# One decoder layer on one core: a Strassen-like pair of K tiles in each column group of the up projection

## The chip, the core and the metric

The kernel runs on one core of a Trainium2 chip. TensorE (PE) multiplies, VectorE (DVE) and ScalarE (ACT) work on SBUF and PSUM, GpSimd (POOL) and the sync engine (SP) here mostly issue DMAs; all DMAs of the core share 16 DMA engines. The metric is the device time of one execution in microseconds; before the change it is 1249.64 us, the median of three runs (1249.38 to 1251.37).

## The reference

One layer on x of shape (1, 256, 2048), float32: two token mixers with an output projection, then a gated MLP with a short causal convolution, then a gated side input. The MLP is what the change touches:

```python
h = rms_norm(x, ffn_norm_g[i])
u = h @ w_up[i]                      # (256, 2048) @ (2048, 11264)
a, g = jnp.split(u, 2, axis=-1)      # 5632 columns each
a = causal_dwconv(a, conv_w[i], conv_b[i])          # width 3, along the sequence
x = x + (jax.nn.gelu(a, approximate=False) * g) @ w_down[i]
gate = jax.nn.sigmoid(rms_norm(x, ple_norm_g[i]) @ w_ple_gate[i])
x = x + gate * (p[i].astype(x.dtype) @ w_ple_proj[i])
```

## The kernel before

**Precision.** Every weight block is loaded as float32 (`raw`), and split into a high part (`hi`, an ACT cast to a shorter float format, line 960) and a low part (`lo = raw - hi`, DVE, line 961). The left operand is split in the same way ahead of time. A product is three matmuls: left-high x hi, left-high x lo, left-low x hi, each with a 128 x 128 left block and a 128 x 512 right block, summed in one PSUM bank.

**The up projection.** 11 column groups q of 512 columns of a and the same 512 of g. A group goes over the 16 K tiles of 128 rows; one K tile is a *unit*: a 512 KB load (2 x 512 columns), a split, and 2 token halves x 2 column halves x 3 = 12 matmuls into four PSUM banks (lines 1248 to 1250). The prediction counts a group's units u0, u1 and so on. In the last unit the banks close one after the other; ACT scales them by `rstd2` into the SBUF tile EZ (`up_rows`, line 860), DVE transposes EZ into Y in two passes (`up_turn`, line 182), and POOL moves Y back into EZ, columns now on partitions, by 16 small DMAs (`move`, line 188). The convolution, the GELU, the product with g, its split and, for some pairs, the sums for the down projection (tile Sp, lines 839 to 846) follow as six jobs, `up_act`, hung behind units of the next group.

**Buffers.** There are 3 load buffers (`RAW`) and 4 slots for split parts (`PARTS`). `run_units` loads ahead as buffers come free (a buffer is free when the low part of its old content is computed) and splits at most 4 units ahead (6 in the down phase, where more tiles are free). All loads are issued by SP, in the program's order: a load that waits holds up those behind it.

**The down projection** runs in two halves of 1024 output columns over 22 pairs of K tiles. Pairs named in `SEVEN` use seven block products instead of eight (`seven`): sums of left blocks come from HBM (`sums`), sums of right blocks are made by DVE. Before the change the first half has eight such pairs (`SEVEN[1:]`), the second nine. In the first half loads may also use tiles that are free by then: EZ, Y (`ring`), the pT tile. The residual x stays in the SBUF tile xs from the mixers until the down projection adds to it.

The order of instructions within each engine is set by a scheduler that goes by estimated times and dependences; it may move a load or a matmul ahead of others that come earlier in the code.

## Time and profile before

| what | us |
|---|---|
| median of the runs | 1249.64 |
| the profiled execution | 1248.63 |
| its span | 1246.5 |
| PE busy | 1238.5 |
| DVE busy | 824.3 |
| ACT busy | 685.7 |
| up projection, first to last matmul start | 431.5 to 910.9 |

The span is what the profile covers of the execution; 2.1 us lie around it. Busy times are sums over the span. A matmul's listed time overlaps that of the next, so the distance between starts is what counts. In rows of a timeline the columns are start, duration, engine, line, operation, tiles and shapes, and in brackets the engine's idle time before the row and what ended it.

### The profile page before, as it was taken

To read this page: it belongs to the slowest core of one execution; us is meant where nothing else is said; L and a number is where in the kernel's file an instruction comes from. 1 tells how busy PE (TensorE), PEld (TensorE's weight loads), DVE (VectorE), ACT (ScalarE), POOL (GpSimd) and SP (SyncE) were. 2 spreads that over 40 slices of the span, in tenths; PEclk is the share of its full clock that TensorE was granted. 3 is DMA by queue.
4 is the path that set the end of the run, shared out by engine and by line. 5 is a ranking of instruction groups with operands and counts; after the bars stand their busy time and mean duration, and the time that the engine had idled before them with its cause. 6 is when DMAs were issued, how large, how long until landed. Compare 5 with 4: busy or idle time off the path is not lost.

```text
span 1246.5 us, 16075 instructions
## 1 busy us (share of the span) xinstructions
PE 1238.5 (99%) x5665; PEld 1043.7 (84%) x5665; DVE 824.3 (66%) x1024; ACT 685.7 (55%) x950; POOL 245.0 (20%) x457
## 2 busy tenths in 40 slices
PE   9999999999999999999999999999999999999998
PEld 7999988888888888888888888888887888888887
DVE  6455566664565655665676576667669998998653
ACT  7565454554554544655565465556556555566542
POOL 2001166512313202202202220220220000050000
PEclk9999999999999999999999999999999999999999
DMA  8766878765667768778877878887897885786560
GB/s 256 196 187 185 231 213 225 199 206 161 185 191 220 215 189 223 206 219 239 233 226 223 231 235 223 233 238 222 216 309 278 281 288 197 251 270 227 176 211 34
DMA packets 133121, 272.67 MB, mean 219 GB/s; under 512 B 14841, under 2 KB 29809, under 8 KB 133041
## 3 DMA queue, kind: packets, MB, share of 16 engines
q1 hardware_dynamic: 117616, 245.99, 65.6%
q0 software_dynamic: 15040, 25.50, 7.2%
q8 instruction: 44, 0.72, 0.2%
q14 instruction: 36, 0.29, 0.1%
q10 hardware_dynamic: 385, 0.16, 0.0%
HBM read 245.89 MB, written 6.83 MB: 203 GB/s over the span
## 4 chain that ended last, share of the span: by engine, by line
PE 92%; DMA 3%; issue 3%; DVE 1%; ACT 0%; POOL 0%; SPq 0%; DVEq 0%; ACTq 0%; POOLq 0%
PE tg L302 13%; PE tg L303 13%; PE tg L304 13%; PE up L1250 12%; PE up L1249 12%; PE up L1248 12%; DMA raw<-in_w_down_dram 2%; PE dnP L1010 1%; PE dnP L1011 1%; PE dnP L1009 1%; PE dn(1, 0)_8622 L1009 1%; PE dn(0, 0)_8614 L1009 1%; PE dn(1, 0)_8622 L1010 1%; PE dn(0, 0)_8614 L1011 1%; PE dn(0, 1)_8618 L1009 1%
## 5 line engine op out<-in xcount | busy, mean ns | idle before, releaser
L961 DVE TENSOR_TENSOR lo<-raw,hi 128x1024 fp32r<-128x1024 f32 x222 | 271.1, 1222 | 177.6 <-ACT hi L960 176.8
L960 ACT CAST hi<-raw 128x1024 fp32r<-128x1024 f32 x222 | 233.4, 1051 | 253.5 <-DMA raw<-in_w_up_dram 109.3
L273 DVE TENSOR_TENSOR lo<-raw,hi 128x1024 fp32r<-128x1024 f32 (+3 forms) x153 | 177.8, 1163 | 154.6 <-ACT hi L271 154.2
L1250 PE MATMUL up<-hi,x2T 128*128 128x512 f32 x704 | 274.0, 389 | 0.0
L1249 PE MATMUL up<-lo,x2T 128*128 128x512 f32 x704 | 273.9, 389 | 0.0
L1248 PE MATMUL up<-hi,x2T 128*128 128x512 f32 x704 | 270.0, 389 | 0.0
L271 ACT CAST hi<-raw 128x1024 fp32r<-128x1024 f32 (+3 forms) x153 | 153.0, 1000 | 155.3 <-PE tg L304 116.4
L303 PE MATMUL tg<-lo,hT 128*128 128x512 f32 (+2 forms) x480 | 181.5, 378 | 0.0
L302 PE MATMUL tg<-hi,hT 128*128 128x512 f32 (+2 forms) x480 | 180.8, 382 | 0.0
L304 PE MATMUL tg<-hi,hT 128*128 128x512 f32 (+2 forms) x480 | 180.3, 377 | 0.0
L1249 PEld LDWEIGHTS up<-lo,x2T 128*128 128x128 f32 x704 | 132.2, 188 | 27.6
L1248 PEld LDWEIGHTS up<-hi,x2T 128*128 128x128 f32 x704 | 132.1, 188 | 27.3
L1250 PEld LDWEIGHTS up<-hi,x2T 128*128 128x128 f32 x704 | 132.1, 188 | 27.3
L188 POOL DMA_DIRECT2D EZ<-Y x176 | 93.3, 537 | 173.0 <-DVE Y L182 98.5
L304 PEld LDWEIGHTS tg<-hi,hT 128*128 128x128 f32 x480 | 90.1, 188 | 12.5
L303 PEld LDWEIGHTS tg<-lo,hT 128*128 128x128 f32 x480 | 90.2, 188 | 11.8 <-DVE lo L273 0.4
L302 PEld LDWEIGHTS tg<-hi,hT 128*128 128x128 f32 x480 | 89.7, 188 | 11.8
L188 POOL DMA_DIRECT2D x3s<-x3s x32 | 16.9, 536 | 168.1 <-PE dn(0, 1)_8618 L1011 159.9
L304 PE MATMUL tg<-hi,catT 128*128 128x512 f32 x128 | 49.9, 390 | 0.0
L302 PE MATMUL tg<-hi,catT 128*128 128x512 f32 x128 | 49.8, 391 | 0.0
L303 PE MATMUL tg<-lo,catT 128*128 128x512 f32 x128 | 49.8, 389 | 0.0
L846 POOL DMA_DIRECT2D sums<-Sp x9 | 5.2, 577 | 224.2 <-DVE Sp L845 224.2
(610 smaller groups left out, 1873.5 us busy)
## 6 DMA issues: line engine op xcount, KB each, us to landing
raw<-in_w_up_dram SPq DMA_DIRECT2D x176, 512.0 KB, 5.0
raw<-in_w_in_dram SPq DMA_DIRECT2D x71, 512.0 KB, 4.2
raw<-in_w_down_dram SPq DMA_DIRECT2D x44, 512.0 KB, 5.5
raw<-in_w_in_dram SPq DMA_DIRECT2D x40, 432.0 KB, 3.8
raw<-in_w_out_dram SPq DMA_DIRECT2D x32, 512.0 KB, 4.7
EZ<-Y POOLq DMA_DIRECT2D x176, 64.0 KB, 5.7
w2raw<-in_w_down_dram SPq DMA_DIRECT2D x20, 512.0 KB, 6.3
S<-sums SPq DMA_DIRECT2D x17, 512.0 KB, 5.3
```

The lines of the kernel that those rows point to most:

```text
L188: pool.dma_start(out=c[32 * b : 32 * b + 32, a::4], in_=y[32 * a : 32 * a + 32, :, b])
L271: act.copy(hi, raw[:, :w])
L273: dve.tensor_sub(lo, raw[:, :w], f32(hi))
L302: pe.matmul(o, ah, hi[:, i, :], start=first, stop=False)
L303: pe.matmul(o, ah, lo[:, i, :], start=False, stop=False)
L304: pe.matmul(o, al, hi[:, i, :], start=False, stop=last)
L960: act.copy(hi, raw)
L961: dve.tensor_sub(lo, raw, f32(hi))
L1009: pe.matmul(o, ah, hi, start=first, stop=False)
L1248: pe.matmul(o, ah, hi[:, n], start=k == 0, stop=False)
L1249: pe.matmul(o, ah, lo[:, n], start=False, stop=False)
L1250: pe.matmul(o, al, hi[:, n], start=False, stop=k == KD - 1)
```

## The change

In ten of the eleven column groups (q > 0) the first two K tiles are taken as one 256-deep block and multiplied with seven block products instead of eight. Left: four sums of blocks of `x2` (made once, in `up_sums`, kept in a part of the tile uC that is not yet in use, `S_up`). Right: the pair's 1 MB of weights is loaded into the first half of xs (`B_up`) by three DMAs, DVE makes sums of its blocks in the second half (`T`), and the pair's splits take three and a half passes of 1024 instead of two. The four units with the products stand at u6 to u9 of the group, which now has 18 units: six plain ones, these four, eight plain ones. Three products go into the group's own banks; four (`upP`) go into banks of their own, are added up by DVE in `z_up` (also in xs), scaled by ACT, and added to EZ by two DVE passes ahead of the transposes.

Since xs is used, x is stored to HBM (`kept_x`, 2 MB) in group 0 and read back by four DMAs in the first down half; until then xs also gives four more load buffers (`x0` to `x3`) for the first 20 units of the down phase. The first down half has seven pairs with seven products (`SEVEN[2:]`) instead of eight. The six jobs of the last group are hung three units apart, and EZ and Y become load buffers later.

```diff
+    kept_x = kp.tile([P, NT, D], F32, name="kept_x")
...
+        S_up = uC[:, KF - KD - 10 : KF - KD - 8].rearrange("p k n -> p (k n)").rearrange("p (i c) -> p i c", c=256)
+        B_up = xs[:, 0]
+        z_up = xs[:, 1].rearrange("p (i c) -> p i c", c=512)
+
+        def move_x(out, i=0):
+            def f():
+                if out:
+                    nc.sync.dma_start(out=kept_x, in_=xs)
+                else:
+                    c = slice(i * 512, (i + 1) * 512)
+                    nc.sync.dma_start(out=xs[:, :, c], in_=kept_x[:, :, c])
+            return f
...
-        def up_turn():
+        def up_turn(q):
             y = Y.rearrange("p (t b c) -> p t b c", t=NT, b=4)
             for t in range(NT):
+                if q > 0:
+                    dve.tensor_add(EZ[:, t], EZ[:, t], xs[:, 1, t * BLK : (t + 1) * BLK])
                 square(y, t, 0, EZ[:, t])
             move(y, Z)
...
-                    room.update(late=2, pT=1, e0=1, e1=1, ring=1)
-                    late.update(gate=gate, free=i + LAST_UP + 1, hi=v[:, 0:2], lo=v[:, 2:4],
+                    room.update(late=2, pT=1, e0=1, e1=1, ring=1, x0=1, x1=1, x2=1, x3=1)
+                    used["pT"] = used["raw"] + 1
+                    late.update(gate=gate, x=i + 20, free=i + 26, hi=v[:, 0:2], lo=v[:, 2:4],
...
+            def seven():
+                B = B_up
+                b22, b21 = B[:, BLK : BLK + 512], B[:, BLK + 512 : 2 * BLK]
+                pb = {}
+
+                def load(j):
+                    c = slice(q * 512, (q + 1) * 512)
+                    nc.sync.dma_start(out=B[:, 0:BLK].rearrange("p (h c) -> p h c", h=2), in_=w[0, :, :, c])
+                    nc.sync.dma_start(out=b22, in_=w[1, :, 1, c])
+                    nc.sync.dma_start(out=b21, in_=w[1, :, 0, c])
+
+                def split1(hi, lo):
+                    part(half(hi, 0), half(lo, 0), half(B, 0))
+
+                T = xs[:, 1]
+
+                def sums(*_):
+                    dve.tensor_sub(T[:, 0:BLK], B[:, 512 : 512 + BLK], B[:, 0:BLK])
+                    dve.tensor_sub(half(T, 2), b22, half(T, 0))
+                    dve.tensor_sub(half(T, 3), b21, half(T, 2))
+
+                def split2(hi, lo):
+                    part(hi, lo, T[:, 0:BLK])
+
+                def split3(hi, lo):
+                    part(hi, lo, T[:, BLK : 2 * BLK])
+
+                def split4(hi, lo):
+                    part(hi, lo, B[:, BLK : 2 * BLK])
...
+                def fn1(hi, lo):
+                    alone(1, left(0, 0), half(hi, 0), half(lo, 0))
+
+                def fn2(hi, lo):
+                    alone(5, S(1), half(hi, 0), half(lo, 0))
+                    alone(7, S(3), half(hi, 1), half(lo, 1))
+
+                def fn3(hi, lo):
+                    alone(6, S(2), half(hi, 0), half(lo, 0))
+                    three(st["b"][1, 0], *left(1, 1), half(hi, 1), half(lo, 1))
+
+                def fn4(hi, lo):
+                    three(st["b"][0, 1], *S(4), half(hi, 0), half(lo, 0))
+                    three(st["b"][0, 0], *left(1, 0), half(hi, 1), half(lo, 1))
+                    z_ = z_up
+                    act.copy(z_[:, 0], pb[1])
+                    dve.tensor_add(z_[:, 1], pb[6], z_[:, 0])
+                    dve.tensor_add(z_[:, 2], pb[7], z_[:, 1])
+                    dve.tensor_add(z_[:, 1::2], pb[5].unsqueeze(1).broadcast_to([P, 2, 512]), z_[:, 1:3])
+                    for t in range(NT):
+                        r = rstd2[:, t : t + 1]
+                        act.activation(z_[:, 2 * t : 2 * t + 2], z_[:, 2 * t : 2 * t + 2], AF.Copy, scale=r)
...
-            return [unit(k) for k in range(KD)]
+            us = [unit(k) for k in range(first, KD)]
+            if q == 0:
+                return us
+            se, sums = seven()
+            with_after(us[2], sums)
+            return us[:6] + se + us[6:]
...
-        us += down(0, "aux", "mm", sums_done(0), add_rest(0), {}, FIRST, SEVEN[1:])
+        with_after(us[6], move_x(True))
+        with_after(us[8], up_sums)
+        us += down(0, "aux", "mm", sums_done(0), add_rest(0), {}, FIRST, SEVEN[2:])
...
-                at = (8, 9, 10, 11, 12, 13) if q < KF // 4 - 1 else (6, 7, 8, 9, 10, LAST_UP)
-                with_after(us[KD * (q + 1) + at[i]], job)
+                if q < KF // 4 - 1:
+                    with_after(plains[q + 1][i], job)
+                else:
+                    with_after(us[first_late + 10 + 3 * i], between(job))
+        for i in range(4):
+            with_after(us[first_late + 34 + 5 * i], between(move_x(False, i)))
```

How the scheduler places it, at three points of the fifth column group (q = 4). Its units are 64 to 79 before the change and 70 to 87 after it; the number behind raw, hi and lo is the unit's.

First SP's queue in the middle of the group, before the change: the loads of u10 to u14.

```order
L946 DMA raw74_0_5439<-in_w_up_dram 128x2x512
L946 DMA raw75_0_5457<-in_w_up_dram 128x2x512
L946 DMA raw76_0_5475<-in_w_up_dram 128x2x512
L946 DMA raw77_0_5493<-in_w_up_dram 128x2x512
L946 DMA raw78_0_5511<-in_w_up_dram 128x2x512
```

And after it, the loads of u10 to u14 again (raw80 to raw84):

```order
L969 DMA raw80_0_5432<-in_w_up_dram 128x2x512
L969 DMA raw81_0_5454<-in_w_up_dram 128x2x512
L969 DMA raw82_0_5472<-in_w_up_dram 128x2x512
L1296 DMA xs_84<-in_w_up_dram 128x2x512
L1297 DMA xs_84<-in_w_up_dram 128x512
L1298 DMA xs_84<-in_w_up_dram 128x512
L969 DMA raw83_0_5549<-in_w_up_dram 128x2x512
L969 DMA raw84_0_5563<-in_w_up_dram 128x2x512
```

The three loads of the next group's pair (into xs) stand between those of u12 and u13.

Second DVE's queue at the start of the group, from the low part of u2 on, before the change:

```order
L961 TENSOR_TENSOR lo66_5320<-raw66_0_5253,hi66_5319 128x1024
L182 STREAM_TRANSPOSE Y_4007<-EZ_4006 128x8x4x32 x2
L961 TENSOR_TENSOR lo67_5360<-raw67_0_5274,hi67_5359 128x1024
L961 TENSOR_TENSOR lo68_5382<-raw68_0_5305,hi68_5381 128x1024
L961 TENSOR_TENSOR lo69_5400<-raw69_0_5323,hi69_5399 128x1024
```

And after it, again from the low part of u2 (lo72) on:

```order
L986 TENSOR_TENSOR lo72_5384<-raw72_0_5317,hi72_5383 128x1024
L855 TENSOR_TENSOR Sf_5356<-Y_4008,Sf_5356 128x128
L885 TENSOR_TENSOR EZ_4007<-EZ_4007,xs_84 128x1024 x2
L986 TENSOR_TENSOR lo73_5429<-raw73_0_5338,hi73_5428 128x1024
L183 STREAM_TRANSPOSE Y_4008<-EZ_4007 128x8x4x32
L1306 TENSOR_TENSOR xs_84<-xs_84 128x1024
L857 TENSOR_TENSOR Sp_5357<-Sf_5356,Sp_5357 128x4x128
L183 STREAM_TRANSPOSE Y_4008<-EZ_4007 128x8x4x32
L986 TENSOR_TENSOR lo74_5451<-raw74_0_5369,hi74_5450 128x1024
L986 TENSOR_TENSOR lo75_5469<-raw75_0_5387,hi75_5468 128x1024
```

Between the low parts of u2 and u4 (lo72, lo74) there are now two adds, a sum of B and the split of Sp besides the two transposes and u3's low part.

Third PE's queue at u4 (unit 74), after the change:

```order
L1275 MATMUL up00_5434<-hi74_5450,x2T0_3577 128x512
L1275 MATMUL up10_5435<-hi74_5450,x2T0_3577 128x512
L1275 MATMUL up01_5436<-hi74_5450,x2T0_3577 128x512
L1275 MATMUL up11_5437<-hi74_5450,x2T0_3577 128x512
L1275 MATMUL upP1_5541<-hi76_5489,x2T0_3577 128x512
L1276 MATMUL up00_5434<-lo74_5451,x2T0_3577 128x512
```

The unit's four matmuls with the high part, and one of u6 (hi76), now stand ahead of the first with the low part; at u13 it is the four alone. Before the change a unit's low part was used from its second matmul on.

More of the change, by code (lines that the diff above doesn't have):

```diff
@@ L45 @@
 FRONT = (8, 4, 4)
-LAST_UP = 11
 @with_exitstack
@@ L902, in may @@
             def may(t):
-                return (t not in ("pT", "ring") or j < late["gate"]) and (t not in ("e0", "e1", "ring") or now[0] > late["free"])
+                return (t not in ("pT", "ring") or j < late["gate"]) and (t not in ("e0", "e1", "ring") or now[0] > late["free"]) and (t[0] != "x" or j < late["x"])
             return sorted((t for t in room if taken.count(t) < room[t] and may(t)), key=lambda t: used.get(t, -1))
@@ L946, in load @@
                     nc.sync.dma_start(out=raw[:, : kb * n].rearrange("p (k n) -> p k n", k=kb), in_=src)
+                    last["load"] = traced()
                     self.raws.append(raw)
@@ L1228, in behind, with between, f @@
             return f
+        def between(hook):
+            def f():
+                with tc.issue_after(last["hi"]), tc.issue_after(last["lo"]), tc.issue_after(last["load"]):
+                    hook()
+            return f
         def with_after(u, hook):
@@ L1237, in up_group, with three, left, S @@
             st = {}
+            first = 2 if q > 0 else 0
+            def three(o, ah, al, hi, lo, start=False, stop=False):
+                pe.matmul(o, ah, hi, start=start, stop=False)
+                pe.matmul(o, ah, lo, start=False, stop=False)
+                pe.matmul(o, al, hi, start=False, stop=stop)
+            def left(k, t):
+                a = x2[:, k]
+                return a[:, t * P : (t + 1) * P], a[:, 256 + t * P : 256 + (t + 1) * P]
+            def S(i):
+                return S_up[:, i - 1, 0:P], S_up[:, i - 1, P:256]
@@ L1246, in fn @@
                             o = st["b"][t, n]
[L1247 to L1250 removed]
+                            three(o, *left(k, t), hi[:, n], lo[:, n], k == first, k == KD - 1)
                             if k == KD - 1:
```

37 lines of the change are left out of this document (26 added, 11 removed).

## The prediction

> **What bounds the kernel now.** I read the profile's page first, then the chain of waits, then windows of single column groups, then the timelines of DVE and ACT at one group's end, and last the DMA rows. The page:
>
> ```profile
> span 1246.5 us, 16075 instructions
> PE 1238.5 (99%) x5665; PEld 1043.7 (84%) x5665; DVE 824.3 (66%) x1024; ACT 685.7 (55%) x950; POOL 245.0 (20%) x457
> PEclk9999999999999999999999999999999999999999
> ```
>
> PE is busy throughout, at the full granted clock. Whether it also never waits, the chain of waits tells (start, duration, what); the same three matmuls stand in each group of the up projection:
>
> ```profile
> 508.74 0.68 PE up L1248 x3
> 552.26 0.68 PE up L1248 x3
> ...
> 856.90 0.68 PE up L1248 x3
> ```
>
> Nine starts lie 43.52 us apart. A group is 192 matmuls, so one costs 43.52 / 192 = 0.2267 us (the 389 ns of the groups' table overlap each other) and a unit of 12 costs 2.72. Not one group waits. The windows (stretch, length, busy PE, PEld, DVE, ACT, POOL, clock, DMA share, GB/s) show what stands behind that:
>
> ```profile
> 552.20:595.80 43.60, 43.60 (x194) 36.12 (x193) 27.87 (x33) 23.88 (x28) 9.06 (x17) 1.00 0.77 227
> 910.90:1030.00 119.10, 117.88 (x520) 97.30 (x519) 106.63 (x119) 69.85 (x81) 8.51 (x16) 1.00 0.83 282
> ```
>
> So a saved matmul in the up projection is worth its 0.2267 us as long as the split weights arrive in time. How much time they have, one unit shows: the group beginning at 606.50, its unit u5 (units counted from 0), due at 606.50 + 5 x 2.72 = 620.10.
>
> ```profile
> 606.50 0.39 PE L1248 MATMUL up<-hi,x2T 128*128 128x512 f32 x1
> 612.13 1.05 ACT L960 CAST hi<-raw 128x1024 fp32r<-128x1024 f32 x1 [1.66 <-PE up L1250]
> 613.22 1.22 DVE L961 TENSOR_TENSOR lo<-raw,hi 128x1024 fp32r<-128x1024 f32 x1 [1.49 <-ACT hi L960]
> 620.32 0.39 PE L1249 MATMUL up<-lo,x2T 128*128 128x512 f32 x1
> ```
>
> The low part is ready at 614.44 and first used at 620.32: a **lead** of 5.88 us. It cannot be larger: the ACT pass waited for PE to free the parts slot of u1 (four slots), at 606.50 + 5.44 = 611.94, and the low part was done 2.50 later. The three units between give 8.16 us; the lead is that, less 2.28.
>
> **The change part by part.** *Matmuls.* Ten groups need 21 products instead of 24 for one pair of K tiles (30 fewer), the first down half 3 more: 27 x 0.2267 = **-6.12 us**.
>
> *DVE and ACT.* Prices, from the groups by shape:
>
> ```profile
> L1057 DVE TENSOR_TENSOR raw<-raw 128x512 f32<-128x512 f32 x8 | 5.5, 689 | 0.1
> L776 DVE TENSOR_TENSOR xs<-tg,xs 128x512 f32<-128x512 f32 x8 | 5.1, 682 | 0.0
> L182 DVE STREAM_TRANSPOSE Y<-EZ 128x1024 f32<-128x1024 f32 x22 | 26.1, 1224 | 5.7 <-ACT EZ L860 5.7
> L872 ACT COPY Y<-EZ 128x1024 f32<-128x1024 f32 x11 | 11.5, 1046 | 1.6 <-DMA EZ<-Y 1.6
> ```
>
> Back to back a 1024 pass takes 1.14 and a 512 pass 0.6 (the overlap is in the next rows: two transposes in 2.37). Per group DVE gains 1.5 splits (1.7), the B sums (1.14 + 2 x 0.6), the three product sums (2 x 0.6 + 1.14) and two adds into EZ (2.3): 8.7 us on 27.9, 36.6 of 42.84. ACT gains about 4.4 (1.5 high passes, one 512 copy, two 1024 passes). DVE at 106.63 of 119.10 kept PE supplied in the down half, so volume alone does not decide: **place** does, twice in each group.
>
> *Place one, the load of u13.* The seven products are u6 to u9 with 3, 6, 6 and 6 matmuls, 4.76 us in all. They use up four parts slots as any units do, so at u10 the three units between give 18 x 0.2267 = 4.08 and the lead is 1.8; at u11 3.2, at u12 4.5. In SP's queue the three loads of the *next* group's B (1.05 MB) now stand ahead of u13's load. They wait until u9's split has read the old B: slot freed at 16.32 (u5's end), so done at 18.8 at the earliest; u13's load follows at about 20.0, when u10's split has freed its buffer. What the DMA engines give in such a stretch, the windows show with POOL's moves of EZ (first row) and without (second); below them the issues of the first stretch (last column: median us to landing) and, over two and a half groups, the landing times of up loads:
>
> ```profile
> 611.00:625.00 14.00, 14.00 (x63) 11.59 (x62) 5.63 (x5) 4.21 (x4) 7.01 (x14) 1.00 1.00 241
> 626.00:650.00 24.00, 24.00 (x107) 19.89 (x106) 19.00 (x25) 16.86 (x21) 0.58 (x1) 1.00 0.73 225
> ...
> raw<-in_w_up_dram SPq DMA_DIRECT2D x5, 512.0 KB, 7.3
> EZ<-Y POOLq DMA_DIRECT2D x14, 64.0 KB, 6.0
> ...
> DMA to landing us min/median/max: 3.8/4.9/7.9
> ```
>
> With moves in flight the engines are full at 241 GB/s; without, 225 / 0.73 = 308 GB/s would fill them. A load alone lands in 3.8, of which 0.52 MB / 308 is 1.7, so 2.1 is fixed and B's data start at 20.9. The moves begin after the transposes:
>
> ```profile
> 604.98 2.41 ACT L860 ACTIVATE EZ<-up,rstd_ffn 128x512 f32<-128x512 f32 x4
> 606.85 2.37 DVE L182 STREAM_TRANSPOSE Y<-EZ 128x1024 f32<-128x1024 f32 x2 [0.52 <-ACT EZ L860]
> 609.14 1.18 DVE L961 TENSOR_TENSOR lo<-raw,hi 128x1024 fp32r<-128x1024 f32 x1
> 609.52 5.30 POOL L188 DMA_DIRECT2D EZ<-Y  x10 [6.26 <-DVE Y L182]
> 619.04 1.08 POOL L188 DMA_DIRECT2D EZ<-Y  x2 [0.25 <-DMA EZ<-Y]
> ```
>
> Transposes end at 609.22, the last move lands at 620.12 + 6.0: 16.9 us later. After the change the transposes end 5 to 8 us later in the group (next place), so moves run until 25 to 28, and about 0.35 of their 1.05 MB is still to come at 20.9. Upper bound: (1.05 + 0.52 + 0.35) MB / 241 GB/s = 8.0, landing 28.9, split (1.05 + 1.22) at 31.2; u13 is at 29.24 and needs the low part after four high matmuls, at 30.15: **1.05 late**. Behind u13's high pass ACT then has the two 1.05 passes that scale the products before u14's: about 0.4 more. Lower bound: 1.57 MB / 308 = 5.1, split at 28.3: 1.8 early, no stall.
>
> [...]
>
> *Place two, the group's end.* DVE had two transposes between u2's and u3's splits. Now it has add, add, u3, transpose, B sum, Sp (0.6), transpose, u4: 7 x 1.14 + 0.6 = 8.6. Begun at T + 0.3 as now (T the group's start; the third eviction), u4 is done at 8.9 and needed at 10.88 + 5 x 0.2267 = 12.0: hidden. But it begins only when u2's split is done. Three load buffers turn over in 3.8 + 1.05 + 1.22 + 0.1 = 6.2 us against 8.16 of PE, so at best 0.66 us of lead is regained per unit, 4.6 between u13 and u2, less the convolution passes in that stretch. A lead of 2 at u2 puts its split at T + 4.35 and u4's at 12.95: **0.9 late**; a lead of 4 leaves 1.1 to spare. I take 0.4.
>
> Sum per group: 0 to 2.4, I take 1.6, near the upper end, since the full window with moves is the nearest row. Groups 1 and 2 live on the 5.88 that they inherit; eight remain: **+12.8 us**.
>
> *Keeping x.* The 2 MB store stands ahead of u6's load in group 0, and B's first load waits for it in SP's queue, with u7's load behind. The rows for a store to HBM (512 KB) and for the one stall of the down half:
>
> ```profile
> 908.43 5.53 DMA sums<-Sp
> ...
> 951.31 1.05 ACT hi L960
> 952.41 0.50 PE dn(1, 0)_7768 L1009
> ```
>
> At 308 GB/s it is 2.1 + 6.8 = 8.9, at the store's rate (0.52 MB in 5.53 - 2.1) 2.1 + 13.7. Loads stand 8.16 + 5.88 = 14 us ahead of PE and need 7, so 7 is spare; u7's load would have waited 5.4 of the 8.9 anyway and B's 0.8 MB adds 2.6: 0 to 6 us, I take **+1**.
>
> *Down.* PE waits 1.2 of 119.1 there, at 952.41, behind DVE. The last group's convolution passes are spread wider, one pair (3.5 x 1.14 + 4 x 0.6 = 6.4 of DVE against 2.3) is plain, and the first fourteen units are plain; x's return less one load of sums is 1.6 MB, 5 us of DMA in a window with 17% of 119 free. -1.2 to +3, I take **-0.7**.
>
> 1248.63 (the profiled execution) - 6.12 + 12.8 + 1 - 0.7 = 1255.6; that execution lies 1.0 under the median of the runs, so **1256.5**.
>
> **The rivals.** *The loads keep up (0.22).* If the moves are through before B arrives, every place is hidden: 1249.6 - 6.1 + 0.5 - 0.7 = 1243, faster. For it: a DMA share of 0.77 over a group, and from u5's to u9's split SP has nothing new to issue, so moves run alone for a while. Against it: the full window, and 1.8 us of lead at u10. It decides when u13's load lands within 9 us of B's issue (30.15 - 1.05 - 1.22 - 18.8). *Stalls of about the saving (0.08):* 0.7 a group, 1247 to 1252. *DVE cannot catch up (0.08):* the adds wait so long that place two costs 2 us beside place one's 1.4, 3.4 x 8 = 27: 1266 to 1273. *That it saves nothing* is excluded: the order has 27 matmuls fewer.
>
> **How the numbers follow.** The forecast (1.1 to 2.4 a group, 1252 to 1264) has 0.62. About 0.2% (2.5 us) is what a measurement here can tell. Faster 0.22, same 0.08, slower 0.70. The forecast's own range is 1252 to 1264; 1242 to 1267 takes in the first rival.
>
> **What would show it.** Groups 1 and 2 near 42.84 us and later ones 44 to 45; ACT's high passes in the middle of a group waiting for up weights, DVE's at u4 with no idle time ahead; a load at u13 of 7 us or more. Wrong, if all groups keep 42.84, or if PE waits mostly at u6 to u10.

## The result, and the profile after

| what | before | after |
|---|---|---|
| median of the runs, us | 1250.94 (14 runs) | 1251.9 (14 runs) |
| the profiled execution, us | 1248.63 | 1249.73 |
| its span, us | 1246.5 | 1248.0 |
| up projection, first to last matmul start, us | 479.4 | 482.3 |

The ratio of the runs is 1.0011, with a 95% interval of 0.9997 to 1.0026: no difference that these runs can tell. The 27 saved matmuls (6.1 us) are there, and something has eaten them.

The page of the changed kernel, its span, its busy times, and the shares of the chain that ended last (the last row is the kernel before's shares):

```profile
span 1248.0 us, 16158 instructions
PE 1237.1 (99%) x5638; PEld 1037.5 (83%) x5638; DVE 900.1 (72%) x1124; ACT 719.1 (58%) x999; POOL 244.1 (20%) x457
...
PE 75%; DVE 12%; DMA 7%; issue 3%; ACT 3%; SPq 0%; ACTq 0%; DVEq 0%
...
PE 92%; DMA 3%; issue 3%; DVE 1%; ACT 0%; POOL 0%; SPq 0%; DVEq 0%; ACTq 0%; POOLq 0%
```

PE alone no longer makes the end: 22% of the chain now runs over DVE, loads and ACT, where it was 4%. The windows of single column groups (stretch, length, busy PE, PEld, DVE, ACT, POOL, clock, DMA share, GB/s; each stretch runs from one group's last matmul to the next one's) say where:

```profile
476.53:519.37 42.84, 42.84 (x190) 35.47 (x189) 30.97 (x33) 28.87 (x34) 8.46 (x16) 1.00 0.75 215
519.37:562.44 43.07, 43.07 (x192) 35.66 (x190) 34.16 (x38) 27.23 (x32) 8.44 (x16) 1.00 0.74 218
562.44:605.28 42.84, 42.84 (x191) 35.42 (x189) 35.42 (x43) 26.97 (x33) 9.03 (x17) 1.00 0.78 228
605.28:650.39 45.11, 44.04 (x190) 35.15 (x189) 36.85 (x44) 28.43 (x34) 9.04 (x17) 1.00 0.77 225
...
782.76:827.05 44.29, 43.51 (x190) 35.24 (x189) 36.64 (x44) 28.18 (x34) 9.04 (x17) 1.00 0.78 228
```

A group without a stall now lasts 189 x 0.2267 = 42.84 us. Groups 1 to 3 (counted from 0) do (one matmul more falls into the second stretch). The six groups from 605.28 to 870.74 take 265.46, which is 8.42 more than 6 x 42.84; with 0.5 us in group 10 and 0.7 in group 0 (of which the kernel before loses 0.2 as well) the stalls are **9.6 us** (the expectations below say 9.5).

They sit at two places, u4 and u13 with its neighbour u14. Group 8, DVE from the low part of u2 to that of u4, then PE at u4 (start, duration, engine, line, operation, tiles; in brackets the idle time ahead and what ended it):

```profile
785.35 1.22 DVE L986 TENSOR_TENSOR lo<-raw,hi 128x1024 fp32r<-128x1024 f32 x1
786.49 0.28 DVE L855 TENSOR_TENSOR Sf<-Y,Sf 128x128 f32<-128x128 f32 x1
786.81 2.36 DVE L885 TENSOR_TENSOR EZ<-EZ,xs 128x1024 f32<-128x1024 f32 x2
789.08 1.22 DVE L986 TENSOR_TENSOR lo<-raw,hi 128x1024 fp32r<-128x1024 f32 x1
790.22 1.24 DVE L183 STREAM_TRANSPOSE Y<-EZ 128x1024 f32<-128x1024 f32 x1
791.38 1.18 DVE L1306 TENSOR_TENSOR xs<-xs 128x1024 f32<-128x1024 f32 x1
792.48 0.68 DVE L857 TENSOR_TENSOR Sp<-Sf,Sp 128x512 fp32r<-128x512 f32 x1
793.08 1.24 DVE L183 STREAM_TRANSPOSE Y<-EZ 128x1024 f32<-128x1024 f32 x1
794.24 2.32 DVE L986 TENSOR_TENSOR lo<-raw,hi 128x1024 fp32r<-128x1024 f32 x2
```

```profile
788.20 0.39 PE L1276 MATMUL up<-lo,x2T 128*128 128x512 f32 x1
...
794.32 0.39 PE L1275 MATMUL upP<-hi,x2T 128*128 128x512 f32 x1
795.48 0.50 PE L1276 MATMUL up<-lo,x2T 128*128 128x512 f32 x1 [0.78 <-DVE lo L986]
```

DVE does not rest for a moment. From the end of u2's low part (786.57) to the end of u4's (about 795.43) it needs 8.86 us. PE, left alone, goes from its first use of u2's low part to that of u4's in two units and four matmuls, 6.35. So a lead of 2.5 us at u2 would hide this; it is 788.20 - 786.57 = 1.63. The bracket shows less than the loss: 795.48 - 794.32 = 1.16 between two starts is 0.93 too much, and the matmuls after it start a little late as well, 1.07 in all. Loss is read from starts.

At u13 the load is what comes last. SP's issues and ACT's passes in the same group:

```profile
797.79 0.54 SPq L1296 DMA_DIRECT2D xs<-in_w_up_dram  x1
803.09 0.33 SPq L1297 DMA_DIRECT2D xs<-in_w_up_dram  x1
803.46 0.43 SPq L1298 DMA_DIRECT2D xs<-in_w_up_dram  x1
804.22 0.55 SPq L969 DMA_DIRECT2D raw<-in_w_up_dram  x1
```

```profile
811.29 1.05 ACT L984 CAST hi<-raw 128x1024 fp32r<-128x1024 f32 x1 [6.35 <-DMA raw<-in_w_up_dram]
812.24 2.19 ACT L1344 ACTIVATE xs<-xs,rstd_ffn 128x1024 f32<-128x1024 f32 x2
814.33 1.98 ACT L984 CAST hi<-raw 128x1024 fp32r<-128x1024 f32 x2
```

The DMA engines in the stretch of u13's load (40 slices of 804.2 to 812.0, busy share in tenths, and the sums):

```profile
DMA  9999699799798999999999999999999999999999
...
DMA packets 1165, 2.24 MB, mean 287 GB/s; under 512 B 192, under 2 KB 192, under 8 KB 1163
```

The engines are full. u13's load, issued at 804.22 behind the next group's pair, is in at 811.2: 7.0 us. Its low part is just in time (a lead of 0.16 us); u14's high pass then waits for the two scaling passes, and PE loses 0.3 us there.

In the first down half PE's wait is gone:

```profile
914.00:1033.00 119.00, 119.00 (x527) 98.54 (x526) 107.21 (x122) 70.48 (x84) 9.07 (x17) 1.00 0.84 292
```

### The profile page after: what moved, and what is told of

It is laid out like the page before. It is cut to its first block, busy times and chain, and to the rows that moved or that the text cites. A ratio compares the mean times of both kernels' runs of the same rounds, so it can differ in the third digit from the quotient of the medians.

```text
span 1248.0 us, 16158 instructions
## 1 busy us (share of the span) xinstructions
PE 1237.1 (99%) x5638; PEld 1037.5 (83%) x5638; DVE 900.1 (72%) x1124; ACT 719.1 (58%) x999; POOL 244.1 (20%) x457
## 4 chain that ended last, share of the span: by engine, by line
PE 75%; DVE 12%; DMA 7%; issue 3%; ACT 3%; SPq 0%; ACTq 0%; DVEq 0%
PE tg L303 13%; PE tg L304 13%; PE tg L305 13%; DMA raw<-in_w_up_dram 6%; DVE lo L986 6%; PE up L1276 5%; PE up L1277 5%; PE up L1275 4%; ACT hi L984 2%; DVE Y L900 1%; DVE Y L183 1%; PE dnP L1036 1%; PE dnP L1037 1%; PE dnP L1038 1%; DVE EZ L885 1%
## 5 line engine op out<-in xcount | busy, mean ns | idle before, releaser
L986 DVE TENSOR_TENSOR lo<-raw,hi 128x1024 fp32r<-128x1024 f32 (+1 forms) x206 | 243.3, 1191 | 96.4 <-ACT hi L984 95.6
L984 ACT CAST hi<-raw 128x1024 fp32r<-128x1024 f32 (+1 forms) x206 | 209.9, 1030 | 155.7 <-DMA raw<-in_w_up_dram 103.3
L1276 PE MATMUL up<-lo,x2T 128*128 128x512 f32 x644 | 252.3, 392 | 4.5 <-DVE lo L986 4.3
L1277 PE MATMUL up<-hi,x2T 128*128 128x512 f32 x644 | 250.9, 390 | 0.0
L1275 PE MATMUL up<-hi,x2T 128*128 128x512 f32 x644 | 201.4, 390 | 0.3 <-ACT hi L984 0.3
L1276 PEld LDWEIGHTS up<-lo,x2T 128*128 128x128 f32 x644 | 120.9, 188 | 35.5 <-DVE lo L986 10.5
L1275 PEld LDWEIGHTS up<-hi,x2T 128*128 128x128 f32 x644 | 120.7, 188 | 26.0 <-ACT hi L984 0.7
L1277 PEld LDWEIGHTS up<-hi,x2T 128*128 128x128 f32 x644 | 120.9, 188 | 24.6
L984 ACT CAST hi<-xs 128x1024 fp32r<-128x1024 f32 (+1 forms) x43 | 40.0, 949 | 56.7 <-DVE xs L1308 36.9
L986 DVE TENSOR_TENSOR lo<-xs,hi 128x1024 fp32r<-128x1024 f32 (+1 forms) x43 | 45.7, 1094 | 17.4 <-ACT hi L984 17.4
L984 ACT CAST w<-raw 128x1024 fp32r<-128x1024 f32 x27 | 28.4, 1054 | 38.1 <-DVE raw L1085 26.8
L305 PE MATMUL tg<-hi,catT 128*128 128x512 f32 x128 | 49.9, 390 | 0.0
```

The costliest lines, as they stand in the source:

```text
L305: pe.matmul(o, al, hi[:, i, :], start=False, stop=last)
L984: act.copy(hi, raw)
L986: dve.tensor_sub(lo, raw, f32(hi))
L1275: pe.matmul(o, ah, hi, start=start, stop=False)
L1276: pe.matmul(o, ah, lo, start=False, stop=False)
L1277: pe.matmul(o, al, hi, start=False, stop=stop)
```

## The experiments

"Idle" is what PE's starts in the up projection lose against 0.2267 us a matmul, summed over the groups; "ratio" is against the kernel before, in the same session, with its 95% interval. A span also holds what its run lost before the up projection, which began at 431.3 to 435.1 us over all these runs, so spans that lie 2 us apart tell little; "idle" is free of that.

| run | idle, us | span, us | ratio |
|---|---|---|---|
| the change | 9.6 | 1248.0 | 1.0011 (0.9997 to 1.0026) |
| the pair's loads behind u15's | 27.9 | 1270.3 | 1.0165 (1.0148 to 1.0181) |
| without the adds | 2.3 | 1249.2 | 0.9986 (0.9972 to 1.0000) |
| both of these | 2.2 | 1246.7 | one run, 1248.44 us |
| down part alone | 0.2 | 1247.3 | one run, 1249.05 us |
| scaling and add in one DVE pass | 34.9 | 1283.4 | 1.0270 (1.0253 to 1.0287) |
| sums of the pair later | 12.9 | 1252.3 | 1.0025 (1.0013 to 1.0037) |
| these two | 20.9 | 1268.8 | 1.0165 (1.0146 to 1.0185) |
| adds on GpSimd | 25.3 | 1267.5 | 1.0146 (1.0127 to 1.0165) |
| half of the moves issued by ACT | 38.9 | 1292.2 | 1.0384 (1.0367 to 1.0402) |
| that, and loads behind u15's | 31.6 | 1285.0 | 1.0286 (1.0272 to 1.0300) |
| that, and one DVE pass | 61.8 | 1312.8 | 1.0528 (1.0513 to 1.0542) |
| kernel before, half of the moves by ACT | 1.1 | 1256.9 | 1.0057 (1.0037 to 1.0077) |
| pair in every other group | 5.0 | 1250.2 | 1.0033 (1.0021 to 1.0044) |
| pair in two groups of three | 8.5 | 1250.5 | 1.0009 (0.9998 to 1.0020) |
| half of the moves left out | 7.3 | 1248.3 | one run, 1249.97 us |
| adds out of the chain | 15.2 | 1256.0 | one run, 1257.92 us |
| **the pair's loads behind u16's** | **0.9** | **1239.4** | **0.9938 (0.9925 to 0.9952)** |
| loads behind u15's, DVE's order held | 15.0 | 1260.7 | 1.0120 (1.0098 to 1.0141) |

**The pair's loads behind u15's.** The first question was whether the loads or DVE's work make the stalls.

```diff
-                def load(j):
-                    c = slice(q * 512, (q + 1) * 512)
+                def load(j, c=slice(q * 512, (q + 1) * 512)):
+                    with tc.issue_after(loads[j - 9]):
...
```

> Edit: the three loads of the next group's pair stand behind u15's load in SP's queue instead of ahead of u13's; nothing is left out. The scheduler answers by setting u3's and u4's low parts ahead of both transposes on DVE. In the changed kernel seven groups (5th to 11th) stall by 0.5 to 1.2 us at u4 and by 0 to 1.2 at u13 and u14, 9.3 us more idle PE than before. Theory A (the pair's 1 MB shares the DMA engines with u13's load, which takes 6.2 to 7.9 us, the lead falls to nothing there and is not regained by u4): u13's load lands within 5 us, the lead of u13's low part is over 1.5 us, no stall at u13, u14 or u4, idle PE in the up projection under 3 us, time 6 to 7 us under the changed kernel, 1244 to 1246. Rival B (DVE's clump at the group's start stalls u4 or its neighbour whatever the loads do): only the 2.6 us at u13 and u14 go, 1249. Rival C (POOL's moves of EZ fill the DMA engines, as the prediction had it): u13's load stays over 6 us without the pair beside it, nothing gained, 1251 to 1252.

Where theory A looked, it was right: u13's load took 4.1 to 5.3 us (issue to high pass) in nine groups of ten, its low part's lead rose to 1.3 us or more there, and u13, u14 and u4 no longer stalled in them. But 27.9 us were idle in this run. The waits of PE in the up projection (for what, us in total, times, longest):

```profile
PE upP L1276 <- DVE lo L986: 9.1, 6, 1.7
PE upP L1275 <- ACT hi L984: 4.2, 8, 0.7
```

They are at the products now, u6 to u9. The scheduler, which goes by its own estimates, had changed DVE's order with the loads: the two transposes and the pair's sums came some 6 us later, close ahead of the products. So the run does not tell loads from DVE's work, and the theories' times all missed.

**Without the adds; both; the down part alone.** The first takes two DVE passes away and leaves SP's queue as it is.

```diff
                 if q > 0:
-                    dve.tensor_add(EZ[:, t], EZ[:, t], xs[:, 1, t * BLK : (t + 1) * BLK])
+                    pass
```

> Leaves out the two DVE adds into EZ ahead of the transposes, so that the four products in banks of their own are missing from the result; the loads stand as in the change. Rival B (clump) and theory A both say that u4's stall goes, since the work ahead of its low part is over 2.3 us shorter and the stall 0.5 to 1.2: idle PE in the up projection 9.5 - 6.2 = 3.3 us, time some 6 us under the changed kernel, 1246. They part at u13: by A its load still takes 6 to 8 us and its low part's lead stays under 1.2 us with stalls of 0 to 1.2 us at u13 and u14; by B alone the lead at u13 would grow with DVE's free time.

> Both edits: the two adds left out (result incomplete as in the run without adds) and the pair's loads behind u15's. If the two places are all that stalls PE, idle PE in the up projection falls to the 0.7 us of group 0 (the store of x) and the span to 1248.0 - 8.7 = 1239.3; if a third place stands behind them (u6 to u10, or the loads as a whole), 2 us or more stay.

Without the adds 7.3 of the 9.6 us are gone, as far as u4 goes as expected. What was not expected: at u13 the stalls went too in most groups, and u13's load took only 4.3 to 5.3 us in eight of them, although the pair's loads stood ahead of it as before. The transposes start 2 to 4 us behind the group's end instead of about 7.4, and in seven groups of ten the moves land at 21 to 23 instead of 28 to 30, so that they are nearly over when the pair and u13 load. In the two groups where u13's load was still slow, 7.2 us in group 3 and 7.6 in group 10, the moves landed at 27; and in the one group of the change where it was fast, 5.2 us in group 1, they landed at 20. So four runs give u13's load, by issue to high pass, in most groups: with neither the pair nor late moves beside it (both edits) 3.9 to 4.1 us, with the pair alone 4.3 to 5.3, with late moves alone (loads behind u15's) 4.1 to 5.3, with both (the change) 6.1 to 7.9. The execution gained little: 2.4 us more than in the change were lost before the up projection, and PE then waited for loads at the start of the down half (2.7 us in one piece):

```profile
PE dn(0, 0)_7943 L1036 <- ACT hi L984: 2.7, 1, 2.7
```

With both edits the idle time is about the same, 2.2, and not 0.7: 0.2 to 0.4 us stay at u15 or u16 of six groups.

> The kernel before with one pair less with seven products in the first down half, and nothing else of the change. Three more matmuls, 0.68 us. The kernel before waits 1.4 us at one place in that half, the changed one nowhere. If one product pair less is what removes it (DVE has 4 us less to do), the span is 1246.5 + 0.7 - 1.4 = 1245.8 and the wait at 952 is gone; if the other parts do it (x0 to x3 as load buffers, the jobs of the last group spread), the wait stays and the span is 1247.2.

```profile
911.00:1030.00 119.00, 119.00 (x527) 98.60 (x526) 101.69 (x113) 67.67 (x77) 8.49 (x16) 1.00 0.84 281
```

The wait is gone with one pair less alone. The span is 1.5 us over the number expected: 2.0 were lost in the first 16 us, behind a first load of x that took 5.22 us here and 4.32 in the profiled execution before, and the stretch behind the up projection gained 1.2 instead of 0.7. That first load took 4.44 us in the change, 5.42 with the pair in every other group and 5.55 without the adds.

**Three ways to give DVE less to do, or later.** One DVE pass per bank for scaling and add (ACT freed); the sums hung behind u4; both; the adds on GpSimd. In the second and third the sums stand behind the splits that read them in the program, so the products use the sums of an earlier pair.

```diff
-            act.activation(EZ[:, t, n * 512 : (n + 1) * 512], b, AF.Copy, scale=rstd2[:, t : t + 1])
+            dve.scalar_tensor_tensor(out=o, in0=b, scalar=r, in1=z_up[:, 2 * t + n], op0=ALU.mult, op1=ALU.add) if q else act.activation(o, b, AF.Copy, scale=r)
...
-            with_after(us[2], sums)
+            with_after(us[4], sums)
...
-                    dve.tensor_add(EZ[:, t], EZ[:, t], xs[:, 1, t * BLK : (t + 1) * BLK])
+                    pool.tensor_add(EZ[:, t], EZ[:, t], xs[:, 1, t * BLK : (t + 1) * BLK])
```

> Nothing left out: the scaling of the banks and the add of the four products become one DVE pass of 512 per bank, so ACT's four passes and DVE's two adds per group go and four DVE passes come (about 0.6 us each, 2.4 for 2.3 on DVE). Theory (the adds push the transposes from 0.35 to 7.4 us behind the group's end, so that the moves of EZ land at 29 instead of 19, meet the pair's loads, and the convolution's last job falls into the next group's start on DVE): transposes start before 6, the stalls at u4 fall below 0.5 us and those at u13 and u14 go, idle PE in the up projection 9.5 to under 6, time 1 to 5 us under the kernel before. Rival (the sheer amount of DVE work at the group's start, 8.6 us between the low parts of u2 and u4, which this edit hardly changes): idle PE stays at 8 to 10, time as the changed kernel's, 1250 to 1252.

> The sums of the pair's blocks are hung behind u4 instead of u2, nothing else; DVE's order now has 7.5 us instead of 8.6 between the low parts of u2 and u4, and the gate product of the convolution ahead of u2's. By the amount of work ahead of u4 its stalls (0.5 to 1.2 us) go and those at u13 and u14 stay: idle PE 9.5 to about 4, time 1246 to 1247. By the lateness of the transposes (they start as late as before, 7 us behind the group's end) the stalls only move, to u5 or to u7 where the sums are first needed: idle PE 8 or more, no gain.

> Both: one DVE pass per bank, and the sums behind u4. In DVE's order u3's and u4's low parts now stand ahead of both transposes. If the work ahead of u4 decides, no stall at u4, idle PE under 3 us, 1243 to 1245. If the lateness of the transposes decides, they start at 8 or later and the run is like the one with the pair's loads late, with stalls at u7 to u9: over 1255.

> The two adds go to GpSimd, nothing is left out; their length there is not known from any row. DVE has 2.3 us less per group, but the transposes wait for GpSimd. By DVE's amount of work the stalls at u4 go (idle PE 9.5 to 3 or 4, 1245 to 1247). By the lateness of the transposes: if a GpSimd pass takes over 2 us, the transposes start no earlier than now, the moves still meet the pair's loads, u13's load stays over 6 us, and 2 to 4 us of stalls at u13 and u14 stay or grow.

All four were slower than the kernel before, and each expectation of a gain failed. With one pass per bank the transposes start at 10 to 14 us, because the passes over the banks must wait for the gate product of the group before (which reads EZ), and that ends only after the group's start; then the products wait for banks and splits. The later sums moved part of the stall from u4 to u8 and u9; the expectation by the lateness of the transposes had it move to u5 or u7. On GpSimd the twenty adds took 2.88 us each in the mean, and DVE's passes beside two of them took longer (last section); u4 stalled by 1 to 4 us.

**Is it EZ's round trip?** From these runs came a second theory: eviction, adds, transposes, moves, convolution and gate product of one group fill the group's time, and the delay is handed on. Four runs spread the moves over a second queue; four others took the pair out of some groups, half of the moves out, or the adds out of the chain.

```diff
-                pool.dma_start(out=c[32 * b : 32 * b + 32, a::4], in_=y[32 * a : 32 * a + 32, :, b])
+                (q2 if b % 2 else pool).dma_start(out=c[32 * b : 32 * b + 32, a::4], in_=y[32 * a : 32 * a + 32, :, b])
...
-            move(y, Z)
+            move(y, Z, act)
```

> Every other one of the 16 moves of EZ is issued by ACT instead of POOL; all of DVE's work stays as in the change, nothing is left out. Theory (the round trip of EZ: eviction, adds, transposes, moves, convolution, gate product, next eviction, is longer than before by the adds and by what they wait for, has filled the group's 43 to 44 us, and each group begins with what the last one left): the moves are out in half the time, land by 24 us behind the group's end instead of 28 to 30, the gate product ends before the group does (now 42 to 43 us behind the last one's end), the transposes start before 5 instead of at 7.4, idle PE in the up projection falls from 9.5 to under 4 us, time 1244 to 1247. Rival 1 (the sheer amount of DVE work ahead of u4): stalls at u4 stay at 0.5 to 1.2 us, no gain, 1250 to 1253. Rival 2 (the engines that move the data, not the issue, set the moves' time): they land at 28 to 30 as now, no gain, 1250 to 1253.

> The same, and the pair's loads behind u15's in SP's queue, which alone made 1270. By the round trip theory that run was slow because the order on DVE put the transposes 13 us behind the group's end; with the moves on two queues the order has both transposes ahead of u4's low part again, so this is as fast as the run with two queues or up to 2 us faster, with a lead at u13 of over 2 us: 1242 to 1246. If late loads are harmful in themselves, over 1255.

> Two queues and one DVE pass per bank in place of scaling and add, which alone made 1284. By the round trip theory it had filled the group's time there too; here the evictions stand between u1's and u3's low parts, the transposes start at 3 to 6 and idle PE is under 5 us: 1243 to 1247. If the passes of DVE over PSUM are harmful in themselves, over 1255.

> The kernel before with every other move issued by ACT, as a control: it has 0.2 us of idle PE in the up projection and 13 us to spare in EZ's round trip, so both theories say no change, within 0.2% of the kernel before, 1248 to 1252.

All failed, the control too. ACT, which makes the high parts, now spends its time issuing (first row: ACT's queue, seven moves in 5.96 us), and PE waits for high parts (second fence, the waits of PE in the first of these runs):

```profile
718.49 5.96 ACTq L189 DMA_DIRECT2D EZ<-Y  x7
```

```profile
PE upP L1275 <- ACT hi L984: 16.8, 14, 2.6
```

The control loses only 1.1 us in the up projection; 8.8 of its 10.4 us are lost behind it, where PE waits 4.2 us in one piece for a high part. These runs tell what eight issues per group cost on an engine that feeds PE, and nothing of the round trip. The other four:

```diff
-            first = 2 if q > 0 else 0
+            first = 2 if q % 2 else 0
...
-            move(y, Z)
+            move(y, Z, (0, 2))
...
+            for t in range(NT if q > 0 else 0):
+                dve.tensor_add(xs[:, 1, t * BLK : (t + 1) * BLK], xs[:, 1, t * BLK : (t + 1) * BLK], xs[:, 1, t * BLK : (t + 1) * BLK])
```

> The pair with seven products in the groups 1, 3, 5, 7 and 9 only (15 matmuls fewer than in the change's ten groups were 30), all else as in the change; complete. Round trip theory (each group with the pair lengthens EZ's round trip and hands the delay on to the next; the first three lost nothing because the delay had not yet built up): a plain group in between, with 13 us to spare, takes the delay away, so no group stalls: idle PE in the up projection under 2 us, of it 0.7 in group 0. Time: 15 x 0.2267 = 3.4 less in the up projection, 0.8 less in the down half, 0.7 more for the store of x: 3.5 us under the kernel before, ratio 0.997. Rival (the amount of DVE work between the low parts of u2 and u4 stalls each group that has it): the five groups stall 0.9 to 1.3 us each as in the change, 5 us in all, time as the kernel before or 1 over.

> The same in the groups 1, 2, 4, 5, 7, 8 and 10, complete. Round trip theory: at most two groups in a row carry the delay, and in the change the second lost nothing: idle PE under 2 us, 21 x 0.2267 = 4.8 less, in all 4.9 under the kernel before, ratio 0.996. Rival: seven groups with 0.9 to 1.3 us each, 6 to 9 us of idle PE, time 1 to 4 us over the kernel before.

> Leaves out 8 of the 16 moves of EZ in each group (half of EZ stays untransposed); POOL issues the rest, ACT has nothing more to do, DVE's work and the adds stay. Round trip theory: moves land 6 us sooner, the transposes start before 5 us behind the group's end, stalls at u4 and u13 go, idle PE under 3 us, span under 1242. Rival (amount of DVE work ahead of u4): stalls at u4 stay at 0.5 to 1.2 us, idle PE over 6.

> The two DVE adds stay, of the same size, but add z to itself behind the transposes instead of z to EZ ahead of them, so that the four products are missing from the result. Round trip theory: as without the adds, transposes start at 2 to 4 us, idle PE under 4.5 us (3.5 without the adds). Rival (amount of DVE work): idle PE as in the change, 8 to 10.

The round trip theory fell. With a plain group in between, the plain groups stalled instead (1.0 to 2.1 us at u8 and u9 in three of them), 5.0 us in all where under 2 was expected; with two groups of three it was again the plain ones, at u4, u8 and u10 (1.2 to 3.0 us); with half the moves, u4 was free but u3, u9 and u13 stalled in single groups, 7.3 us where under 3 was expected; with the adds out of the chain 15.2 us were lost, mostly at u14, because the scheduler had put adds and sums right between the low parts of u13 and u14. The rival, DVE's amount of work at u4, fell with it: that work is the same in most of these runs, and the stalls wandered from u3 to u14. What the stalls that were read had in common was 3 to 9 us of DVE work (3.4 ahead of u14 in the last of them, 8.9 ahead of u4 in the change) at a place where the lead was smaller than that work asks for.

**The loads alone.** One run was wanting: later loads with DVE's order kept. One unit later than in the first experiment, the scheduler leaves DVE's order as it is in the change but for a few rows in the groups 0 and 1. The run beside it keeps the loads behind u15's and holds both transposes ahead of u3's low part.

```diff
-                    last["load"] = traced()
+                    last["load"] = loads[j] = traced()
...
+                    with tc.issue_after(loads[j - 8]):
+                        nc.sync.dma_start(out=B[:, 0:BLK].rearrange("p (h c) -> p h c", h=2), in_=w[0, :, :, c])
+                        nc.sync.dma_start(out=b22, in_=w[1, :, 1, c])
+                        nc.sync.dma_start(out=b21, in_=w[1, :, 0, c])
```

> The pair's loads stand behind u16's load (the last two behind u17's) in SP's queue, one unit later than in the run that placed them behind u15's; complete. In this place the scheduler leaves DVE's and ACT's order in the groups 2 to 10 as the change has it, so this moves the loads alone. By the leads (u13's load shares the DMA engines with the pair, the lead is used up there, and DVE's clump of 8.7 us needs 2.4 us of lead at u2 but finds 1.4 to 2.1): u13's load takes about 5 us, its low part's lead is over 1.5 us, the lead at u2 grows over 2.4, and the stalls at u13, u14 and u4 all go: idle PE in the up projection 9.5 to under 3 us, time 5 us or more under the kernel before, ratio under 0.997. By DVE's amount of work alone: only the 2.6 us at u13 and u14 go, 0.5 to 1.2 us at u4 stay in seven groups, ratio 0.998 to 1.000. If the pair harms whichever loads it stands beside: stalls of 0.5 us or more at u16 to u0 in place of those, no gain.

> The pair's loads behind u15's, as in the run that took 1270, and DVE made to take both transposes ahead of u3's low part; complete. If that run was slow because the order on DVE had moved the transposes to 13 us behind the group's end and with them the rest, this one is free of it: transposes start before 6, idle PE under 4 us, time 3 us or more under the kernel before. If loads behind u15's are slow in themselves, over 1255 again.

The first of the two beats both kernels: 1240.92 us (five runs, 1240.25 to 1242.56) against 1248.9, ratio 0.9938 with 0.9925 to 0.9952. Its groups in the windows, and all that PE waits for in the up projection (0.7 us by the starts, at u3 of group 2):

```profile
562.68:605.52 42.84, 42.84 (x190) 35.48 (x189) 36.20 (x44) 27.45 (x34) 9.03 (x17) 1.00 0.74 231
...
776.68:819.52 42.84, 42.84 (x191) 35.47 (x189) 36.96 (x45) 28.30 (x34) 9.04 (x17) 1.00 0.78 236
```

```profile
PE up L1276 <- DVE lo L986: 0.4, 1, 0.4
```

DVE is as busy as in the change (36.96 us of group 8 against 36.64), and from group 3 on PE loses under 0.1 us in all. Group 8 again, DVE from u2's low part on, and PE's first uses of the low parts of u2 and u4:

```profile
778.13 1.22 DVE L986 TENSOR_TENSOR lo<-raw,hi 128x1024 fp32r<-128x1024 f32 x1
779.26 0.29 DVE L855 TENSOR_TENSOR Sf<-Y,Sf 128x128 f32<-128x128 f32 x1
779.46 2.36 DVE L885 TENSOR_TENSOR EZ<-EZ,xs 128x1024 f32<-128x1024 f32 x2
...
785.73 1.24 DVE L183 STREAM_TRANSPOSE Y<-EZ 128x1024 f32<-128x1024 f32 x1
786.89 2.32 DVE L986 TENSOR_TENSOR lo<-raw,hi 128x1024 fp32r<-128x1024 f32 x2
```

```profile
782.34 0.39 PE L1276 MATMUL up<-lo,x2T 128*128 128x512 f32 x1
...
788.69 0.39 PE L1276 MATMUL up<-lo,x2T 128*128 128x512 f32 x1
```

The same instructions in the same order take 8.73 us (779.35 to 788.08), and u2 now starts with a lead of 782.34 - 779.35 = 2.99 instead of 1.63, so 0.61 is left at u4. The lead comes from u13. Its load, the first of the four in the next row, is issued at 796.95, 1.2 us earlier in the group than in the change, and is in at 801.4, 4.5 us after its issue instead of 7.0. The pair's first load goes out behind u16's:

```profile
796.95 7.36 SPq L969 DMA_DIRECT2D raw<-in_w_up_dram  x4
804.37 0.60 SPq L1296 DMA_DIRECT2D xs<-in_w_up_dram  x1
```

```profile
801.44 1.05 ACT L984 CAST hi<-raw 128x1024 fp32r<-128x1024 f32 x1 [3.29 <-DMA raw<-in_w_up_dram]
803.36 1.05 ACT L984 CAST hi<-raw 128x1024 fp32r<-128x1024 f32 x1 [0.88 <-PE up L1277]
804.31 2.19 ACT L1344 ACTIVATE xs<-xs,rstd_ffn 128x1024 f32<-128x1024 f32 x2
```

One thing besides the loads has changed, against the expectation: in the groups 2 to 9 the scheduler now puts u14's high pass ahead of the two scaling passes (second and third row), and u14's matmuls on PE in another order. That alone can take away the 0.3 us at u14, and no run shows it apart. It does not explain u4: u15's high pass stands behind both scaling passes in either order, and the lead of its low part in group 8 is 3.1 us here and 1.6 in the change. The transposes still start 5.7 to 6.7 us behind the group's end, about 1 us earlier than in the change, and harm nothing, which speaks against the round trip once more.

The run beside it stalls at u3, where the held order puts adds, sum and transposes, by 1.0 to 2.6 us in eight groups (u3 is needed a unit sooner than u4), and by 4.1 us at the start of the down half. With the loads behind u15's in both, the order alone moved the loss from the products to u3. That the loads behind u15's are harmless in themselves was not shown: every run with them had another order on DVE. The least that was lost with them is the 2.2 us of the run with both edits, which leaves out the adds.

## Why the prediction was wrong

The time, 1251.9, lies in the wide range that takes in the first rival (1242 to 1267), and 0.1 us under the forecast's own (1252 to 1264). The forecast, slower by 6.9 us, does not hold: it was 1.0 us, and not distinguishable from nothing. By the terms of the sum, on the profiled executions:

| term | predicted, us | measured, us |
|---|---|---|
| 27 matmuls | -6.1 | -6.1 |
| stalls per group | 8 x 1.6 = +12.8 | 7 x 1.27 = +8.9 |
| keeping x | +1 | +0.5 |
| down | -0.7 | -2.0 |
| sum | +7.0 | +1.3; the span grew by 1.5 |

The time behind the up projection's last matmul shrank by 1.5 us although two of the three additional matmuls of the down half stand there, which makes -2.0 for the rest. From group 1 on the groups without a stall last exactly 189 x 0.2267 us, so the matmuls are worth what the prediction said. Both places are where the prediction put them, with the engines it named, and the early groups run free as it said (three, not two). The step that failed is the **size of the stalls**, the term of 8 x 1.6: it came out 30% lower, 3.9 us. The sum is a small difference of large terms, so this, with 1.3 us more gained in the down half than foreseen, made 7.0 into 1.5.

*Place one was priced too high*: 1.2 us a group, measured 0.4, about half of it at u14 behind the scaling passes. The working let all three loads of the pair wait until u9's split, at 18.8. The first, half of the data, does not: it went out at 797.79, 15.0 us into group 8, and only the other two waited, until 20.3. So 0.5 MB less stood ahead of u13's load, which took 6.1 to 7.9 us in nine groups and not 8.9; and the full engines gave 287 GB/s, not the 241 of the row that the upper bound was worked out from.

*Place two was priced too low*: 0.4, measured 0.9. "A lead of 2 at u2 ... 0.9 late" is exactly what happened (the leads at u2 were 1.4 to 2.1); the value taken was one between that and a lead of 4.

*The two were added as if they were separate causes.* They are one: the load that is late at u13 takes the lead, DVE and three load buffers win back about 2 us of it at most until u2, and DVE's clump there finds too little. Moving the pair's loads, with DVE's order kept, removed both. The prediction had the link in its working, as a lead regained by 0.66 us a unit at best (measured some 0.3: from 0.1 at u14 of four groups to 1.6 to 2.0 at the next u2), and in its first rival, where every place is hidden once the loads keep up. Its sum still priced the second place apart from the first.

*Down* was right in its direction and too small: one pair less with seven products removes the wait, shown alone, and it goes whole (1.4 us by the starts); 0.4 us more are gone behind the last matmul. *Keeping x* cost 0.5 us at u7 of group 0; with the first pair's loads later it is gone.

Of the rivals, stalls of about the saving came true by its time, 1247 to 1252, which had a chance of 0.08; it lay between two cases that had 0.84 and deserved more. That it fits so well is in part luck: it had 0.7 us a group, and the runs show 1.27 in seven groups, in part made good by the down half. "The loads keep up", with 1243, 6.3 us under the kernel before, was a fair price for the kernel with the pair's loads four loads later, whose span is 7.1 us under the kernel before's.

## What to carry to other kernels

A stall is charged where the lead runs out, not where it was used up: before shortening the work ahead of it, follow the lead back to the last place at which it fell. Transfers that are not needed soon belong behind those that are, in a stretch where nothing waits for a load; here that took the ratio to the kernel before from 1.0011 to 0.9938, some 9 us, and the four attempts to give the engine that was seen last less to do, or to do it later or elsewhere, made it worse. Where a scheduler sets the order, an edit in one queue can reorder another, so compare the orders before reading a run as a test of the edit.

## What the runs showed of the hardware

**DVE's passes beside GpSimd's adds took longer.** With the adds on GpSimd (first row, two in 5.76 us; the twenty of the run took 2.88 each in the mean), DVE's two passes beside them took 2.03 and 2.89 us, where passes of the same lines and shapes took 1.22 and 0.68 in the change:

```profile
794.15 5.76 POOL L885 TENSOR_TENSOR EZ<-EZ,xs 128x1024 f32<-128x1024 f32 x2 [22.90 <-DVE Sf L855]
```

```profile
795.61 2.03 DVE L986 TENSOR_TENSOR lo<-raw,hi 128x1024 fp32r<-128x1024 f32 x1 [1.48 <-PE up L1277]
797.57 2.89 DVE L857 TENSOR_TENSOR Sp<-Sf,Sp 128x512 fp32r<-128x512 f32 x1
```

The second pass ends at 800.46, 0.55 us behind the end of the adds (799.91). What held the two passes up was not shown.

**Behind a wait of 2.73 us PE ran at about half its rate for 3.2 us.** The stall at 795.48 in the change cost 1.07 us, of which 0.93 lie ahead of that start; the start behind it comes 0.34 us later instead of 0.2267. Behind the wait of 2.73 us in the run without the adds, matmuls started 0.43 us apart until 930.2, and 0.23 from there on:

```profile
927.04 0.79 PE L1036 MATMUL dn(0, 0)_7943<-hi,uA 128*128 128x512 f32 x1 [2.73 <-ACT hi L984]
927.63 0.63 PE L1036 MATMUL dn(0, 1)_7947<-hi,uA 128*128 128x512 f32 x1
928.06 0.63 PE L1036 MATMUL dn(1, 0)_7951<-hi,uA 128*128 128x512 f32 x1
```

The mean granted clock of that run is 1.00 from 910 to 920, 0.84 from 920 to 930, 0.99 from 930 to 940 and 1.00 from 940 to 950. As an estimate from the starts, half the clock from 927.04 to 930.2 alone would give 0.85 and 0.99. What ends the slow stretch was not shown. In the run with the pair's loads behind u15's, where the longest wait of PE listed from 431 to 936 is 1.7 us, the mean granted clock of the whole span is 0.994; in the change, where the longest listed from 431 to 914 is 0.9 us, it is 1.00.
